# Dealing the projections and filter pieces evenly over the attention steps of a two-block kernel

## The chip, the cores and the metric

The kernel runs on one core of one Trainium2 chip. The metric is the device time of one execution in microseconds (us). Before the change three runs took 1946.99, 1946.99 and 1947.81 us, a median of 1946.99 us. The execution that the profiler took lasted 1947.53 us, with a span of 1945.8 us from the first to the last instruction.

## The reference

Four layers run in sequence over 512 tokens of width 1024: two layers of a first block and two of a second. The change touches the first block alone, so both of its layers. One such layer computes:

```python
h = rms_norm(x, pre_norm[l], NORM_EPS)
q, k, v, z_a, u_h, z_h, g_a, g_h = jnp.split(h @ w_in[l], splits, axis=-1)
o = diff_attention(q, k, v, lam, rel_bias)          # 4 heads, softmax(c=0) - lam * softmax(c=1)
o = rms_norm(o, subln[l], SUBLN_EPS) * (1.0 - lam_init)
y_a = o * silu(z_a)
hv, hx1, hx2 = jnp.split(short_conv3(u_h, conv_w[l], conv_b[l]), 3, axis=-1)
filt = hyena_filters(S, ...)                        # a small sine network, then a spectrum
z = fft_long_conv(hv, filt[:, 0], bias0) * hx1
z = fft_long_conv(z, filt[:, 1], bias1) * hx2
y_h = z * silu(z_h)
m = sigmoid(g_a) * (y_a @ w_pa[l]) + sigmoid(g_h) * (y_h @ w_ph[l])
x = x + rms_norm(m @ w_out[l], post_norm[l], NORM_EPS)
```

Two things matter here. The columns of `h @ w_in` are independent of one another, and so are the filters, so both can be computed at any time before they are used. The gates `sigmoid(g_a)` need neither the attention nor the convolution.

## The kernel before

Matmuls are done in three passes on split operands (`mm3`, L261 to L263): a high and a low part of each side. A projection of 128 columns (`projT`) is therefore 8 x 3 = 24 matmuls of 128x512, and its weights come through `wchunk`: a DMA on SP's queue into one of two buffers `wr` (L283), a copy to `wh` on ACT (L269) and the remainder to `wl` on DVE, or on POOL for every third one (L270).

`attention1` walks over 16 steps: 4 heads `hd` times 4 query tiles `i`. A step computes the logits of its two softmaxes into `lg` (L669, L670, two buffers), adds the bias and takes the row maximum on DVE (L673), negates it (L677), takes exponentials on ACT (L679), and combines the two on DVE (L682 to L686) into a weight tile `p`. The transposes of `p` (L586), their copy `wt` on ACT (L588) and the product with the values (`av`, L590) are kept in the list `later` and issued one step afterwards. After a head's fourth step `finish` normalises the head: squares on ACT (L634), a small sum on DVE (L636), a power on POOL (L637), a product on DVE (L638), four transposes on PE (L641), the gating on DVE (L642), and the split of the result into `yh` and `yl` (L269 on ACT, L270 on POOL).

Beside these steps three generators are advanced, one `next` at a time:

- `filters` (called `flt`): for each of four groups (o, g) four pieces with small matmuls (L505, L506) and two pieces of `bank` products, 24 pieces in all, plus three at the start that are taken before the attention. Every group ends in four stores `hd` on SP's queue (L558, L559).
- `proj(hd)` (called `nxt`): the key and the query projection of the next head and the gate `z_a` of this head, three pieces; only the gate for the last head. The keys and queries of head 0 are made before the first step.
- `hyena_v` (called `zv`): a first `next` that only allocates `z`, then four projections with a short convolution (L710 to L712), then four gate projections with one ACT pass each (L837). What is left of it runs after the last step.

`NX[i]` is the number of `nxt` pieces in query tile `i`; `ZS` lists, by step number `4 * hd + i`, when `zv` is advanced.

Behind the attention come `hyena` (two long convolutions through transforms: sums and differences L751 to L755, transposes L761, forward products into `lg`, elementwise work L784 to L801, inverse products L820), and, dealt into it, `branch_a`: products of `w_pa` with `y_a`, in the order of the heads, added on DVE at L854.

The text order of the Python code is not the order on the engines. The tile framework replays the program on its own timeline and writes out one order for each engine; each engine then runs its list strictly in order, so that an instruction that waits holds up all that is behind it on that engine. PSUM has two `acc` buffers, one `fl`, two `lg`, one `tr`, one `ft` and one `av`.

Of the kernel before, what the change touches and what calls it, by code (L numbers as in the profile page):

```python
# [171 lines left out]
class Kern:  # L172
# [389 lines left out]
    def attention1(self, l, h, v, flt, zv):  # L562
# [19 lines left out]
        def values(hd, i, w, po):  # L582
            def run():
                pw = self.ps("tr", (P, 4, P))
                for kt in range(4):
                    nc.tensor.transpose(pw[:, kt], w[:, kt * P:(kt + 1) * P], self.ident)  # L586
                wt = self.T("wt", (P, 4, P))
                nc.scalar.activation(wt, pw, AF.Copy)  # L588
                for kt in range(4):
                    nc.tensor.matmul(po[:, i], wt[:, kt], v[:, kt, hd * P:(hd + 1) * P],  # L590
                                     start=kt == 0, stop=kt == 3)
            return run
# [32 lines left out]
        def finish(hd, po, s0):  # L625
            def run():
                za = gate[hd]

                e0 = self.sm(4, "e0")
                nc.vector.scalar_tensor_tensor(e0, s0, 1e-5, s0, op0=MUL, op1=MUL)  # L630
                ss = self.sm(4, "hss")
                o = self.T("o", (P, 4, P))
                for i in range(4):
                    nc.scalar.activation(o[:, i], po[:, i], AF.Square, accum_out=ss[:, i:i + 1])  # L634
                r = self.sm(4, "hr")
                nc.vector.scalar_tensor_tensor(r, ss, 1.0 / P, e0, op0=MUL, op1=ADD)  # L636
                nc.gpsimd.tensor_tensor(r, r, self.mhalf[:, :4], op=ALU.pow)  # L637
                nc.vector.tensor_tensor(o, po, self.bc(r), op=MUL)  # L638
                pt = self.ps("tr", (P, 4, P))
                for i in range(4):  # L640
                    nc.tensor.transpose(pt[:, i], o[:, i], self.ident)  # L641
                nc.vector.scalar_tensor_tensor(za, pt.rearrange("p i t -> p (i t)"), subs, za, op0=MUL, op1=MUL)  # L642
                self.split(za, yh[:, hd], yl[:, hd], pool=True)
            return run
# [4 lines left out]
            nc.gpsimd.memset(la[b].bitcast(F32), 0.0)  # L649
            nc.gpsimd.memset(lb[a].bitcast(F32), 0.0)  # L650

        NX, ZS = (1, 2, 0, 0), (8, 12, 13, 14, 15)
        for _ in proj(-1):
            pass
        for hd in range(4):
            nxt = proj(hd)
            bias = self.bias_tile(hd)
            po = self.ps("av", (P, 4, P))
            s0 = self.sm(4, "s0")
            for i in range(4):  # L660
                ts = slice(i * P, (i + 1) * P)
                for _ in range(2):
                    next(flt, None)
                mx, s = self.sm(2, "mx"), self.sm(1, "s1")
                pp = []
                for c in range(2):
                    q, k, kl = qk[hd][c]
                    ps = self.ps("lg")
                    nc.tensor.matmul(ps, q[:, ts], k, start=True, stop=False)  # L669
                    nc.tensor.matmul(ps, q[:, ts], kl, start=False, stop=True)  # L670
                    p = self.T("p")
                    b0 = 511 + 128 * i
                    nc.vector.tensor_tensor_reduce(  # L673
                        out=p, in0=ps, in1=bias[:, b0:b0 - S if i else None:-1], op0=ADD, op1=MAX,
                        scale=1.0, scalar=-3.0e38, accum_out=mx[:, c:c + 1])
                    pp.append(p)
                nc.vector.tensor_scalar(mx, mx, -1.0, None, op0=MUL)  # L677
                for c in range(2):
                    nc.scalar.activation(pp[c], pp[c], AF.Exp, bias=mx[:, c:c + 1],  # L679
                                         accum_out=s0[:, i:i + 1] if c == 0 else s)  # L680
                r1 = self.sm(1, "r1")
                nc.vector.reciprocal(r1, s)  # L682
                cc = self.sm(1, "cc")
                nc.vector.scalar_tensor_tensor(cc, s0[:, i:i + 1], nlam, r1, op0=MUL, op1=MUL)
                w = pp[0]
                nc.vector.scalar_tensor_tensor(w, pp[1], cc, w, op0=MUL, op1=ADD)  # L686
                for f in later:
                    f()
                for _ in range(NX[i]):
                    next(nxt, None)  # L690
                for _ in range(ZS.count(4 * hd + i)):
                    next(zv)
                later = [values(hd, i, w, po)] + ([finish(hd, po, s0)] if i == 3 else [])
# [922 lines left out]
```

## Time and profile before

| | |
|---|---|
| median of 3 runs | 1946.99 us |
| profiled execution | 1947.53 us, span 1945.8 us |
| PE busy | 1882.4 us (97%) |
| PE weight loads busy | 1566.2 us (80%) |
| DVE busy | 1290.4 us (66%) |
| ACT busy | 890.0 us (46%) |
| POOL busy | 648.2 us (33%) |
| chain that ended last | PE 65%, DVE 11% |

PE is the engine that is nearly always busy; the other four are not. The shares are means over the whole span. For a change that touches two stretches of it (the attention of layer 0, 60 to 200 us, and that of layer 1, 530 to 680 us), the views by stretch tell more: they give the busy time of each engine, the number of instructions, the TensorE clock that was granted (1.00 is the full 2.4 GHz, 0.50 would be 1.2 GHz throughout) and the share of the DMA engines.

### The profile page before, as it was taken

What the parts mean: (1) busy time and instruction counts of PE and PEld (TensorE: products, weight loads), DVE (VectorE), ACT (ScalarE), POOL (GpSimd) and SP (SyncE); (2) the same over time, 40 slices, a digit from 0 to 9 for tenths busy, and PEclk for the clock granted to TensorE, in tenths of its full rate; (3) what the DMA queues carried; (4) which work ended last, traced back from release to release, by engine and by line L of the source; (5) the groups of instructions that cost most, each with busy time, mean ns of one, the idle gap of its engine ahead of it and who ended that gap; (6) DMA issues with size and microseconds to landing.
All of it is one profiled execution on the core that took longest, in us unless ns stands there. A gap on an engine that the chain in (4) does not pass through costs nothing.

```text
span 1945.8 us, 26168 instructions
## 1 busy us (share of the span) xinstructions
PE 1882.4 (97%) x9632; PEld 1566.2 (80%) x9632; DVE 1290.4 (66%) x2278; ACT 890.0 (46%) x1732; POOL 648.2 (33%) x555
## 2 busy tenths in 40 slices
PE   8997999999998899999999999999999999999998
PEld 5886888888787687888888777788889887778886
DVE  5887698634697868873558866667334886666732
ACT  4765322234475632233346254466334625446631
POOL 2544344433243634442235314211013532421111
PEclk9999999999999999999999999999999999999999
DMA  5331433324323242323432231112333223121232
GB/s 180 106 121 64 146 109 98 105 91 163 117 86 113 73 170 89 112 93 104 135 123 75 81 101 39 63 44 77 138 127 107 75 87 95 38 63 47 83 130 87
DMA packets 88393, 192.35 MB, mean 99 GB/s; under 512 B 28258, under 2 KB 38499, under 8 KB 88265
## 3 DMA queue, kind: packets, MB, share of 16 engines
q1 hardware_dynamic: 69592, 184.84, 29.0%
q10 hardware_dynamic: 17376, 3.67, 1.0%
q0 software_dynamic: 1296, 2.16, 0.4%
q8 instruction: 76, 1.25, 0.3%
q14 instruction: 53, 0.43, 0.1%
HBM read 172.28 MB, written 18.37 MB: 98 GB/s over the span
## 4 chain that ended last, share of the span: by engine, by line
PE 65%; DVE 11%; issue 3%; ACT 2%; DMA 1%; POOL 1%; ACTq 1%; POOLq 0%; DVEq 0%; SPq 0%
PE acc L261 11%; PE acc L263 11%; PE acc L262 11%; PE fl L261 5%; PE fl L262 5%; PE fl L263 5%; PE av L1166 2%; DVE u L1373 1%; DVE s L1371 1%; PE av L261 1%; PE av L262 1%; PE av L263 1%; PE lg L1470 1%; DVE wl L270 1%; PE av L820 1%
## 5 line engine op out<-in xcount | busy, mean ns | idle before, releaser
L269 ACT ACTIVATE wh<-wr 128x1024 fp32r<-128x1024 f32 (+3 forms) x268 | 256.1, 956 | 467.5 <-PE acc L262 231.3
L261 PE MATMUL acc<-u,wh 128*128 128x512 f32 x1000 | 400.6, 401 | 3.2 <-DVE o L704 1.9
L262 PE MATMUL acc<-u,wh 128*128 128x512 f32 x1000 | 400.4, 400 | 0.0
L263 PE MATMUL acc<-u,wl 128*128 128x512 f32 x1000 | 397.8, 398 | 0.0
L270 POOL TENSOR_TENSOR wl<-wr,wh 128x1024 fp32r<-128x1024 f32 (+3 forms) x86 | 187.2, 2177 | 555.2 <-ACT wh L269 460.2
L270 DVE TENSOR_TENSOR wl<-wr,wh 128x1024 fp32r<-128x1024 f32 (+3 forms) x182 | 213.3, 1172 | 184.8 <-ACT wh L269 182.6
L261 PEld LDWEIGHTS acc<-u,wh 128*128 128x128 f32 x1000 | 190.8, 191 | 46.1 <-issue 3.3
L263 PEld LDWEIGHTS acc<-u,wl 128*128 128x128 f32 x1000 | 190.9, 191 | 43.6 <-issue 4.9
L262 PEld LDWEIGHTS acc<-u,wh 128*128 128x128 f32 x1000 | 190.8, 191 | 39.8 <-issue 2.3
L261 PE MATMUL fl<-u,wh 128*128 128x512 f32 x312 | 124.4, 399 | 0.0
L263 PE MATMUL fl<-u,wl 128*128 128x512 f32 x312 | 122.7, 393 | 0.0
L262 PE MATMUL fl<-u,wh 128*128 128x512 f32 x312 | 122.2, 392 | 0.0
L263 PE MATMUL acc<-wh,u 128*128 128x512 f32 (+1 forms) x212 | 79.3, 374 | 0.3
L262 PE MATMUL acc<-wl,u 128*128 128x512 f32 (+1 forms) x212 | 79.4, 374 | 0.0
L261 PE MATMUL acc<-wh,u 128*128 128x512 f32 (+1 forms) x212 | 77.8, 375 | 0.4 <-ACT u L269 0.2
L261 PEld LDWEIGHTS fl<-u,wh 128*128 128x128 f32 x312 | 58.7, 188 | 12.8 <-issue 1.6
L679 ACT ACTIVATE p<-p,mx 128x512 f32<-128x512 f32 x64 | 45.7, 717 | 49.9 <-DVE mx L677 49.9
L263 PEld LDWEIGHTS fl<-u,wl 128*128 128x128 f32 x312 | 58.6, 188 | 12.1
L262 PEld LDWEIGHTS fl<-u,wh 128*128 128x128 f32 x312 | 58.7, 188 | 12.0 <-issue 0.8
L324 ACT ACTIVATE sq<-x 128x512 f32<-128x512 f32 x40 | 25.2, 631 | 61.4 <-DVE x L1569 38.4
L793 POOL TENSOR_TENSOR w<-w,ab 128x256 f32<-128x256 f32 x32 | 33.5, 1047 | 57.9 <-DVE w L792 53.1
L902 POOL TENSOR_TENSOR m<-m,u 128x512 f32<-128x512 f32 x16 | 24.7, 1546 | 66.3 <-DVE m L901 66.3
(610 smaller groups left out, 4473.8 us busy)
## 6 DMA issues: line engine op xcount, KB each, us to landing
wr<-in_win SPq DMA_DIRECT2D x88, 512.0 KB, 3.4
wr<-in_xin SPq DMA_DIRECT2D x64, 512.0 KB, 3.4
wr<-in_xout SPq DMA_DIRECT2D x32, 512.0 KB, 3.5
hd<-f SPq DMA_DIRECT2D x32, 256.0 KB, 2.4
hs<-hd SPq DMA_DIRECT2D x32, 256.0 KB, 3.4
wr<-in_wout SPq DMA_DIRECT2D x16, 512.0 KB, 3.5
xd<-x SPq DMA_DIRECT2D x12, 512.0 KB, 2.9
x<-xd SPq DMA_DIRECT2D x12, 512.0 KB, 3.9
```

The source lines that it names most:

```text
L261: mm(ps, l[0], r[0], start=first, stop=False)
L262: mm(ps, l[0], r[1], start=False, stop=False)
L263: return mm(ps, l[1], r[0], start=False, stop=last)
L269: nc.scalar.activation(hi, src, AF.Copy)
L270: (nc.gpsimd if pool else nc.vector).tensor_tensor(lo, src, hi.bitcast(F32), op=SUB)
L324: self.nc.scalar.activation(self.T("sq"), self.xt(i)[:, h * S:(h + 1) * S], AF.Square, scale=1.0 / math.sqrt(D), accum_out=self.ms2[i][:, ...
L679: nc.scalar.activation(pp[c], pp[c], AF.Exp, bias=mx[:, c:c + 1], accum_out=s0[:, i:i + 1] if c == 0 else s)
L793: nc.gpsimd.tensor_tensor(a[:, 0], a[:, 0], b[:, 1], op=ADD)
L820: nc.tensor.matmul(ps[:, k], Y[j][:, k, cs], iv[:, j, (k + 1) // 2 % 2], start=j == 0, stop=j == 1)
L902: nc.gpsimd.tensor_tensor(m, m, ma[f // 4][:, f % 4], op=ADD)
L1166: mm(po[:, ts], v[hd // 4][:, k, (hd % 4) * P:(hd % 4 + 1) * P], w[:, k], start=k == 0, stop=k == i)
L1371: nc.vector.tensor_tensor(t, a[:, j, c:].unsqueeze(2).to_broadcast([64, r, c]), m[:, j:j + 1, :c].to_broadcast([64, r, c]), op=MUL)
```

## The change

Three tuples of numbers change. With `NX = (1, 1, 1, 0)` each of the first three query tiles of a head gets one of the three projections (key, query, gate), where the second tile used to get two. With the new `ZS` the four convolution projections go to steps 3, 7, 11 and 13, and two of the four gate projections to steps 14 and 15; the other two still follow the last step. So each of the 16 steps now holds exactly one projection of 24 matmuls. `FS = (2, 1, 2, 1)` deals six filter pieces, one whole group, to each head, where two pieces a step used to use up all 24 in steps 0 to 11.

```diff
-        NX, ZS = (1, 2, 0, 0), (8, 12, 13, 14, 15)
+        NX, ZS, FS = (1, 1, 1, 0), (3, 3, 7, 11, 13, 14, 15), (2, 1, 2, 1)
         for _ in proj(-1):
             pass
         for hd in range(4):
@@
             for i in range(4):
                 ts = slice(i * P, (i + 1) * P)
-                for _ in range(2):
+                for _ in range(FS[i]):
                     next(flt, None)
```

What this makes of the engines' lists is shown at three places. The first is PE in layer 0, between the logits of steps 10 and 11 (head 2). `lg` are logits, `av` the values' product, `fl` and `ft` filter sums, `acc` a projection. Before:

```order
L669 MATMUL lg_1632<-qk_1025,qk_1145 128x512
L670 MATMUL lg_1632<-x_246,qk_1145 128x512
L669 MATMUL lg_1637<-qk_1026,qk_1146 128x512
L670 MATMUL lg_1637<-x_246,qk_1146 128x512
L590 MATMUL av_913<-v_292,wt_1394 128x128 x4
L505 MATMUL fl_1198<-fwh_1186,a_46_255 128x256
L505 MATMUL ft_1212<-fwh_1186,a_46_255 128x256
L669 MATMUL lg_1713<-qk_1025,qk_1145 128x512
L670 MATMUL lg_1713<-x_246,qk_1145 128x512
```

The same place now, without the repeated rows of the projection `acc_1597` and of the filter sums:

```order
L669 MATMUL lg_1568<-qk_1032,qk_1112 128x512
L670 MATMUL lg_1568<-x_246,qk_1112 128x512
L669 MATMUL lg_1573<-qk_1033,qk_1113 128x512
L670 MATMUL lg_1573<-x_246,qk_1113 128x512
L261 MATMUL acc_1597<-u_94,wh_1599 128x512
...
L505 MATMUL fl_1450<-fwh_1321,a_46_255 128x256
...
L590 MATMUL av_908<-v_292,wt_1385 128x128 x4
L505 MATMUL ft_1528<-fwh_1321,a_46_255 128x256
...
L669 MATMUL lg_1663<-qk_1032,qk_1112 128x512
L670 MATMUL lg_1663<-x_246,qk_1112 128x512
```

Between the two steps' logits stood one product with the values and two filter matmuls; now a whole projection of 24 matmuls stands there with eight filter matmuls and the product with the values.

The second place is PE in layer 1 at the end of the attention: the last product with the values, and the transposes of `finish` for head 3 (`tr<-ident,o`). Before, with `acc_6061` and `acc_6126` as projections:

```order
L590 MATMUL av_5844<-v_4399,wt_6165 128x128 x4
L261 MATMUL acc_6061<-u_4092,wh_6063 128x512
...
L263 MATMUL acc_6126<-u_4093,wl_6129 128x512
L641 MATMUL tr_6183<-ident,o_6174 128x128 x4
L261 MATMUL acc_6192<-u_4092,wh_6194 128x512
```

Now, with `acc_6409` and `acc_6460` as branch products with head 3 of `y_a`, and `lg_6369` as the first forward product of the convolution:

```order
L263 MATMUL fl_6474<-u_4093,wl_6477 128x512
L590 MATMUL av_5828<-v_4399,wt_6187 128x128 x4
L586 MATMUL tr_6225<-ident,p_6167 128x128 x4
L761 MATMUL ft_6594<-ident,qd_6585 128x128 x2
L761 MATMUL ft_6594<-ident,qd_6591 128x128 x2
L590 MATMUL av_5828<-v_4399,wt_6230 128x128 x4
L641 MATMUL tr_6248<-ident,o_6239 128x128 x4
L761 MATMUL tr_6358<-ident,qd_6342 128x128 x2
L761 MATMUL tr_6358<-ident,qd_6348 128x128 x2
L261 MATMUL acc_6409<-u_4538,wh_6404 128x512
L261 MATMUL acc_6460<-u_4538,wh_6404 128x512
L261 MATMUL lg_6369<-sd_6337,x_6331 128x256
```

48 matmuls of two projections (and twelve filter matmuls) stood between the last product with the values and the transposes, and 96 more of four projections behind them; now the transposes follow the product directly, and the branch products that need them follow after four transposes.

The third place is SP's queue in layer 0 at the same point: `x` is the next layer input, loaded into the buffers that the filters' tables leave, `hd` the last filter stores, `wr` weights, `hs` the first filter loads of the convolution. Before:

```order
L283 DMA wr_2189<-in_win 128x1024
L915 DMA x_3926<-in_x 128x1024 x2
L558 DMA hd_223<-f_1701 128x512
L559 DMA hd_225<-f_1677 128x512
L558 DMA hd_224<-f_1706 128x512
L559 DMA hd_226<-f_1678 128x512
L283 DMA wr_2303<-in_wpa 128x1024
L770 DMA hs_2265<-hd_219 128x512
```

And now:

```order
L283 DMA wr_2189<-in_win 128x1024
L283 DMA wr_2303<-in_wpa 128x1024
L283 DMA wr_2375<-in_win 128x1024
L915 DMA x_3926<-in_x 128x1024
L283 DMA wr_2428<-in_win 128x1024
L915 DMA x_3926<-in_x 128x1024
L558 DMA hd_223<-f_2052 128x512
L559 DMA hd_225<-f_1964 128x512
L558 DMA hd_224<-f_2057 128x512
L559 DMA hd_226<-f_1965 128x512
L283 DMA wr_2545<-in_wpa 128x1024
L770 DMA hs_2265<-hd_219 128x512
```

Three weight loads moved ahead of the input load and the filter stores.

## Rows read from the trace of the kernel before

**Rows 1.** The page's first part: busy us, share of the span, instructions.

```profile
span 1945.8 us, 26168 instructions
...
PE 1882.4 (97%) x9632; PEld 1566.2 (80%) x9632; DVE 1290.4 (66%) x2278; ACT 890.0 (46%) x1732; POOL 648.2 (33%) x555
```

**Rows 2.** Busy time by stretch of the span; the first line names the columns.

```profile
core 0: us, PE busy (x) PEld busy (x) DVE busy (x) ACT busy (x) POOL busy (x), PEclk, DMA share, GB/s
60.00:130.00 70.00, 70.00 (x378) 60.15 (x377) 61.48 (x118) 47.39 (x94) 36.53 (x32) 1.00 0.32 107
130.00:200.00 70.00, 53.98 (x285) 45.02 (x284) 54.16 (x106) 39.96 (x92) 34.18 (x32) 0.90 0.25 81
250.00:330.00 80.00, 76.86 (x409) 65.14 (x408) 74.99 (x108) 20.46 (x27) 38.62 (x30) 1.00 0.31 99
530.00:570.00 40.00, 40.00 (x206) 32.76 (x205) 35.35 (x68) 29.37 (x52) 14.91 (x15) 1.00 0.27 91
570.00:680.00 110.00, 95.05 (x522) 79.36 (x521) 92.70 (x171) 67.69 (x157) 54.72 (x51) 0.97 0.27 88
```

**Rows 3.** Timeline of PE, layer 0: start, length, instruction, idle before it.

```profile
158.17 0.47 PE L669 MATMUL lg<-qk,qk 128*128 128x512 f32 x1 [1.74 <-DVE mx L673]
...
173.78 0.51 PE L669 MATMUL lg<-qk,qk 128*128 128x512 f32 x1 [3.06 <-DVE mx L673]
...
175.57 0.79 PE L261 MATMUL acc<-u,wh 128*128 128x512 f32 x1 [0.86 <-DVE o L704]
...
180.43 0.63 PE L263 MATMUL acc<-u,wl 128*128 128x512 f32 x1
180.85 0.45 PE L261 MATMUL acc<-u,wh 128*128 128x512 f32 x1
...
181.37 0.39 PE L263 MATMUL acc<-u,wl 128*128 128x512 f32 x1
181.60 0.39 PE L261 MATMUL acc<-u,wh 128*128 128x512 f32 x1
```

**Rows 4.** Timeline, layer 1, from the last product with the values to head 3's split.

```profile
672.95 1.05 PE L590 MATMUL av<-v,wt 128*128 128x128 f32 x8
...
674.04 0.28 ACT L634 ACTIVATE o<-av 128x128 f32<-128x128 f32 x1 [0.29 <-PE av L590]
...
675.95 0.88 DVE L636 SCALAR_TENSOR_TENSOR hr<-hss,e 128x4 f32<-128x4 f32 x1
...
676.90 1.40 POOL L637 TENSOR_TENSOR hr<-hr,mhalf 128x4 f32<-128x4 f32 x1
...
678.34 0.69 DVE L638 TENSOR_TENSOR o<-av,hr 128x512 f32<-128x512 f32 x1
...
686.70 0.60 PE L641 MATMUL tr<-ident,o 128*128 128x128 f32 x4
...
687.91 0.74 DVE L642 SCALAR_TENSOR_TENSOR o<-tr,subs,o 128x512 f32<-128x512 f32 x1
...
688.68 0.63 ACT L269 ACTIVATE u<-o 128x512 fp32r<-128x512 f32 x1 [0.29 <-DVE o L642]
...
690.22 1.47 POOL L270 TENSOR_TENSOR u<-o,u 128x512 fp32r<-128x512 f32 x1
```

**Rows 5.** The same in layer 0, to the product on DVE.

```profile
217.33 1.06 PE L590 MATMUL av<-v,wt 128*128 128x128 f32 x8
...
220.19 2.37 DVE L636 SCALAR_TENSOR_TENSOR hr<-hss,e 128x4 f32<-128x4 f32 x1
...
224.17 0.69 DVE L638 TENSOR_TENSOR o<-av,hr 128x512 f32<-128x512 f32 x1 [0.93 <-POOL hr L637]
```

**Rows 6.** Groups on DVE, 55 to 700 us: count, busy us, mean ns, idle before.

```profile
L270 DVE TENSOR_TENSOR u<-f,u 128x512 fp32r<-128x512 f32 x32 | 32.5, 1026 | 1.0 <-ACT u L269 0.7
...
L557 DVE TENSOR_TENSOR f<-f,f 128x512 f32<-128x512 f32 x16 | 18.1, 1156 | 2.9 <-POOL f L556 2.9
```

**Rows 7.** Timeline of DVE, layer 0: two splits of a filter tile.

```profile
128.92 0.69 DVE L270 TENSOR_TENSOR u<-f,u 128x512 fp32r<-128x512 f32 x1
...
187.24 2.82 DVE L270 TENSOR_TENSOR u<-f,u 128x512 fp32r<-128x512 f32 x1
```

**Rows 8.** SP's own queue, end of layer 0's attention: start, length, issue.

```profile
189.54 16.20 SPq L283 DMA_DIRECT2D wr<-in_win  x2
208.39 0.81 SPq L915 DMA_DIRECT2D x<-in_x  x2
...
214.16 0.45 SPq L283 DMA_DIRECT2D wr<-in_wpa  x1
```

## The prediction

> **What bounds the kernel now.** I read the first part of the page first: PE is busy for 97% of the span, DVE for 66% [rows 1]. So only what PE loses can be won, some 63 us in all, and the question is how much of that lies where the change works. The view by stretch answers it [rows 2]. In the first half of layer 0's attention (60 to 130 us) PE has no gap. In the second half (130 to 200 us) it is busy for 53.98 of 70 us and the granted clock is 0.90. Layer 1 repeats this: full from 530 to 570 us, then 95.05 of 110 us from 570 to 680 us at a clock of 0.97. The reader is to see that one attention has two unlike halves, and that no other engine is full in the poor half: DVE is busy for 54.16 of 70 us there. The timeline of PE shows what a gap looks like [rows 3]: logits that wait for the row maximum of the step before (idle 1.74 and 3.06 us), with nothing else in PE's list to go on with. And it shows what follows a gap: the projection that begins at 175.57 us runs at first with 0.42 us from one matmul to the next (180.43 to 180.85 us) and from then on with 0.23. That is the clock at 1.2 GHz and at 2.4 GHz; the twelve spacings up to 180.85 us took 5.28 instead of 12 x 0.23 = 2.76 us, so this slow stretch cost 2.5 us.
>
> **What is there to win.** Idle: 70 - 53.98 = 16.0 us in layer 0 and 110 - 95.05 = 15.0 us in layer 1. Clock: a mean of 0.90 over 70 us is 2 x 0.10 x 70 = 14 us at half clock, of which half is lost while PE is busy, 7 x 0.77 = 5.4 us; in layer 1 2 x 0.03 x 110 = 6.6 us at half, 3.3 x 0.86 = 2.8 us. Sum: 31.0 + 8.2 = 39.2 us [rows 2]. Nothing that PE computes is removed, so this is the ceiling of the gain.
>
> **Part one: the steps themselves.** The moved work is matmuls that need no attention result. At 0.23 us (the full-clock spacing) a projection is 24 x 0.2275 = 5.5 us. Before, steps 2, 3, 6, 7, 10 and 11 issue none and steps 1, 5, 9 and 12 issue two; now every step has one, and between the logits of steps 10 and 11 PE's list has 24 projection matmuls where it had two filter matmuls and one product with the values. PE's work in layer 0's attention is 70 + 53.98 - 5.4 = 118.6 us, plus the two gates that move in, 2 x 5.5 = 10.9 us: 129.5 us, 8.1 us a step. DVE has 61.48 + 54.16 = 115.6 us, plus at most two weight remainders of some 1.3 us: 118.2 us, 7.4 us a step. So PE becomes the slower of the two in every step, by 0.7 us, and a gap needs a delay beyond that. The halves that are dense already show how close this can go: DVE at 61.48 of 70 us (88%) and at 35.35 of 40 us (88%), with PE full both times [rows 2]. Now DVE must hold 118.2 / 129.5 = 91%. Bounds: if it can, no idle is left; if it stops at 88%, the stretch takes 118.2 / 0.88 = 134.3 us and leaves 4.8 us. I take the middle, 2.4 us a layer, 4.8 us for both.
>
> What moves with a projection: its weight load on SP's queue, its copy on ACT, its remainder on DVE or POOL. ACT is at 39.96 of 70 us and POOL at 34.18 [rows 2], so these stay hidden; if that cover went, a weight chunk would stand 1 to 2 us late before one projection. The filter pieces are spread to steps 12 to 15 and with them the last four stores, which the second convolution alone needs, tens of us later. On SP's queue the old order made the branch weights wait behind the input load and the stores, from 208.39 to 214.16 us [rows 8]; now they stand ahead of both, and behind the waiting input load stands one weight load, for a projection after the first forward products. I take 0 for this; between 0 and 1 us.
>
> **Part two: the end of the attention.** Here the change adds waits. The gates that moved were PE's work while head 3 was finished. After the last product with the values (672.95 to 674.0 us) the squares start at 674.04 and the product on DVE ends at 679.03 us, 5.0 us later; the transposes waited in PE's own list until 686.70 [rows 4], 13.7 us after the product began, and nobody minded. From the transposes' start to the end of the copy (688.68 + 0.63) are 2.6 us more, and the low part on POOL took 1.47 us. In layer 0 the first part took from 218.39 to 224.86, 6.5 us [rows 5], since DVE's small sum took 2.37 us.
>
> Now in layer 1's list the transposes come directly behind the last product. PE will stand for about 5.0 us (3 at the least: four squares of 1.2, then 0.2, 1.0 and 0.7; 6.5 at the most, as in layer 0). Queued behind them on PE are four transposes (0.35 us), two branch products with head 3 and the forward products of the convolution; DVE's gating and all of the convolution's elementwise work wait for those. The branch products then wait 2.6 - 0.35 = 2.2 us for head 3's high part, and the next ones some 0.3 us (up to 1.6) for the low part. Before the last product PE waits 0.3 to 0.6 us for the copy of its transposes. Sum 7.8 us. Behind so long a stand I expect the half clock, as behind the 3.06 and 0.86 us of rows 3: 2.5 us. Layer 1 pays 10.3 us (6 to 13).
>
> In layer 0 the list has eight projection matmuls and four transposes between the last product and the transposes of `finish`: 1.8 + 0.35 = 2.2 us of cover. So 5.0 - 2.2 = 2.8 us, then the same 2.2 and 0.3 us, and the half clock half the time, 1.3 us: 6.6 us (2 to 10).
>
> On that half clock the Trainium skill says the same in a stronger form ("TensorE: Matmul & The Clock Gate", section "Part 1: The HAM clock gate"): the slow clock is the default state, and only activity releases it. By that rule the stand in layer 1 costs its 2.5 us for certain, and the sum stays; if the clock held, the forecast would be some 4 us lower. Rows 3 agree with it.
>
> **Part three: the convolution behind it.** Its first forward products used to come after 26 (layer 0) and 28 (layer 1) branch and projection matmuls of this stage; now 44 come first in both, which leaves 18 and 16 matmuls less to run beside its elementwise chain: 4.1 and 3.7 us. From 250 to 330 us DVE is busy for 74.99 of 80 us while PE already loses 3.1 us [rows 2], so cover has worth there. Bounds 0 and 7.8 us; I take half, 3.9 us, since DVE also gets two or three of its instructions done earlier.
>
> **The sum.** Won 39.2; paid back 4.8 + 10.3 + 6.6 + 3.9 = 25.6. Net 13.6 us: 1947.5 - 13.6 = 1933.9 us against the profiled execution, which stands 0.5 us above the median. Against the median 1933.4 us.
>
> **The rivals.**
>
> *The end is covered after all.* If DVE and ACT are well ahead of PE at the last step, and the finish takes 3 us, layer 0 has no stand (3.0 - 2.2 = 0.8) and the clock holds in both; paid back are then 2.4 us between the steps, 0.5 + 3.0 + 2.2 + 0.3 = 6.0 at layer 1's end, 0.8 + 2.2 + 0.3 = 3.3 at layer 0's and nothing in the convolution, 11.7 us: 1947 - 27.5 = 1919 us. For it: PE is now the slower engine in every step, so the others run ahead. Against it: the chain was 5.0 and 6.5 us long in the two cases that the trace has [rows 4, 5].
>
> *DVE becomes the bound.* The moved filter pieces bring POOL's sums and DVE's two-operand instructions into the half with three heads to finish. Such instructions stretch beside POOL: the split of a filter tile took 0.69 us once and 2.82 us another time, with a mean of 1.03 over 32; the sixteen differences had a mean of 1.16 [rows 6, 7]. The excess is 32 x 0.34 + 16 x 0.47 = 18 us for both layers. If it doubled, 9 us a layer would put DVE at 127 of 129.5 us, and the gaps between steps would come back at half their size, 19.6 us: 39.2 - 19.6 - (25.6 - 4.8) = -1 us, no change, about 1948 us. The skill's rule speaks for this rival: "GPSIMD Engine Reference", section "1. Specifications", has GpSimd share its SBUF interfaces with VectorE and names two-input instructions as those that contend. The rows agree that it happens; they don't show that moving the pieces makes more of it. Against the rival: the first half held 16 of the 24 pieces with PE full.
>
> *The end costs more than the steps give: slower.* One place, the end of each attention: after the last product PE has only work that waits for head 3. At its upper bounds layer 1 loses 0.6 + 6.5 + 2.2 + 1.6 + 2.5 = 13.4 us and layer 0 2.2 less, 11 us, and the convolution its whole 7.8 us, 32 us in all. This decides when the steps win less than 32 of the 39.2 us; with half of them won it is 1947 + 32 - 19.6 = 1959 us. For it: PE's list of layer 1 has nothing between the last product and the transposes. Against it: the lists give layer 0 eight matmuls, and the steps look dense.
>
> **How the numbers follow.** The forecast 0.58 (its own range 1924 to 1943 us), the covered end 0.22, DVE as the bound 0.13, the costly end 0.07. The range, 1918 to 1945 us, leaves out the best half of the second case, most of the third and the fourth. About 0.2% (3.9 us) is what a measurement of this kernel tells from no change: below 1943.1 us lie the forecast, the second case and a little of the third: faster 0.85; same 0.09; slower 0.06.
>
> **What would show it.** Right: from 130 us to the end of layer 0's attention, and from 570 us in layer 1, logits no longer wait 1 to 3 us for the maximum and the clock is 1.00; PE stands 3 to 6 us at the transposes of `finish` at the end of layer 1's attention, less in layer 0, with a dip of the clock behind it. Wrong: logits that still wait inside heads 1 to 3 (DVE bound), or no stand at the two ends (then it is faster than I say), or new idle of over 4 us a layer inside the convolution.

## The result, and the profile after

The changed kernel takes 1932.85 us (median of 4 runs, 1931.28 to 1934.41); the kernel before took 1946.99 us on the same chip (4 runs, 1946.33 to 1947.81). The ratio is 0.9927, 95% interval 0.9910 to 0.9944. The forecast was 1933.4 us. The profiled execution lasted 1933.28 us, 14.3 us less than the one before.

The first part of the page, beside [rows 1]: the same matmuls on PE, the same busy time, a shorter span.

```profile
span 1931.5 us, 26186 instructions
...
PE 1882.2 (97%) x9632; PEld 1565.8 (81%) x9632; DVE 1294.6 (67%) x2278; ACT 890.4 (46%) x1732; POOL 653.9 (34%) x555
```

The stretches of [rows 2] again; the columns are those named there (length, busy us of PE, its weight loads, DVE, ACT and POOL, granted clock, DMA):

```profile
60.00:130.00 70.00, 68.40 (x368) 57.55 (x368) 63.17 (x114) 46.44 (x94) 33.17 (x30) 1.00 0.29 99
130.00:200.00 70.00, 68.78 (x380) 58.28 (x379) 60.35 (x112) 44.76 (x96) 39.74 (x35) 1.00 0.36 116
250.00:330.00 80.00, 74.24 (x381) 63.13 (x380) 68.75 (x101) 18.23 (x24) 38.26 (x30) 0.94 0.31 99
...
570.00:680.00 110.00, 103.87 (x550) 87.63 (x549) 93.59 (x158) 66.75 (x142) 60.16 (x52) 0.97 0.36 118
```

The second half of layer 0's attention, where PE was busy for 53.98 of 70 us at a clock of 0.90, is now dense at 1.00. The convolution behind it lost: 74.24 of 80 us at 0.94, where it was 76.86 at 1.00. And layer 1's stretch is better only by half.

To see where the time went, the same view cut at the work's own marks: from the first to the last logits, on to the first forward product of the convolution, on to its last inverse product; layer 0, then layer 1. Before:

```profile
60.20:185.10 124.90, 113.55 (x612) 96.66 (x611) 102.17 (x206) 78.31 (x171) 57.85 (x52) 0.96 0.30 99
185.10:241.90 56.80, 52.13 (x266) 43.81 (x265) 37.57 (x56) 24.40 (x45) 24.72 (x20) 0.97 0.42 135
241.90:375.80 133.90, 130.76 (x687) 111.25 (x686) 113.89 (x160) 36.41 (x49) 60.83 (x48) 1.00 0.33 107
535.20:659.60 124.40, 113.01 (x604) 94.71 (x602) 105.97 (x204) 81.87 (x175) 56.85 (x51) 0.97 0.28 92
659.60:716.20 56.60, 53.04 (x276) 44.17 (x275) 39.23 (x64) 25.23 (x46) 21.61 (x19) 1.00 0.43 149
716.20:852.80 136.60, 132.51 (x686) 112.81 (x685) 113.95 (x160) 36.27 (x48) 62.97 (x48) 0.98 0.32 105
sum 633.20, PE 595.00 PEld 503.42 DVE 512.77 ACT 282.48 POOL 284.82; mean PE 99.17 PEld 83.90 DVE 85.46 ACT 47.08 POOL 47.47
```

After:

```profile
60.10:192.40 132.30, 129.48 (x703) 109.22 (x702) 116.55 (x216) 87.30 (x183) 68.19 (x61) 1.00 0.32 106
192.40:230.40 38.00, 35.82 (x196) 30.00 (x194) 24.05 (x45) 16.11 (x34) 11.47 (x9) 1.00 0.49 158
230.40:367.80 137.40, 130.39 (x665) 110.92 (x665) 115.75 (x161) 35.55 (x48) 63.22 (x49) 0.96 0.32 104
527.40:663.00 135.60, 129.76 (x687) 109.26 (x686) 118.38 (x219) 90.55 (x187) 67.88 (x57) 0.97 0.31 102
663.00:707.50 44.50, 39.63 (x212) 33.08 (x210) 27.53 (x49) 18.13 (x37) 15.44 (x13) 0.94 0.46 148
707.50:841.10 133.60, 130.15 (x665) 110.96 (x665) 116.34 (x161) 35.59 (x47) 63.02 (x49) 0.97 0.31 103
sum 621.40, PE 595.24 PEld 503.45 DVE 518.61 ACT 283.22 POOL 289.22; mean PE 99.21 PEld 83.91 DVE 86.43 ACT 47.20 POOL 48.20
```

The first column after the stretch is its length, so length minus PE is what PE stood:

| PE idle, us | before | after |
|---|---|---|
| layer 0: steps / end / convolution | 11.4 / 4.7 / 3.1 | 2.8 / 2.2 / 7.0 |
| layer 1: steps / end / convolution | 11.4 / 3.6 / 4.1 | 5.8 / 4.9 / 3.4 |
| sum | 38.2 | 26.2 |

The six stretches are 11.8 us shorter, and that is the idle time alone: PE's busy sum is the same (595.00 and 595.24 us). The clock gave nothing. Time at half clock, 2 x (1 - clock) x length summed over views of 10 us up to 960 us, was 27 us and is 31 us; it left layer 0's steps and came back in the convolutions and at layer 1's end. Of the other 2.5 us of the 14.3, 2.3 lie in layer 2 (485.3 us from its first transposes to layer 3's, now 483.0), where the engines' lists are the same in both kernels. The four runs of experiments 1 to 4, also with that list, took 484.2 to 485.8 us for it: that part is scatter, not the change.

The largest stand left between the steps, on PE, then on DVE (the second of its two differences once more by itself), then on POOL (start, length, instruction, idle before it):

```profile
649.40 0.79 PE L669 MATMUL lg<-qk,qk 128*128 128x512 f32 x1 [4.49 <-DVE mx L673]
```

```profile
644.23 4.51 DVE L557 TENSOR_TENSOR f<-f,f 128x512 f32<-128x512 f32 x2
...
645.91 2.83 DVE L557 TENSOR_TENSOR f<-f,f 128x512 f32<-128x512 f32 x1
...
648.66 0.68 DVE L673 CUSTOM_DVE_ANT_0 p<-lg,bias 128x512 f32<-128x512 f32 x1
```

```profile
642.91 2.53 POOL L556 TENSOR_TENSOR f<-f,f 128x512 f32<-128x512 f32 x2 [6.94 <-DVE f L552]
645.40 2.79 POOL L270 TENSOR_TENSOR wl<-wr,wh 128x1024 fp32r<-128x1024 f32 x1
```

Logits wait for a row maximum, as in [rows 3], and the maximum stands behind two filter differences in DVE's list, which took 4.51 us. The same pair in the kernel before stood at 657.69 us:

```profile
657.69 2.36 DVE L557 TENSOR_TENSOR f<-f,f 128x512 f32<-128x512 f32 x2
```

So it did not move into the late heads; it became 2.15 us longer, since POOL, when it had done its two sums, now had a weight remainder to make beside the second difference. The rows show how. The second difference ended at 648.74 us, 0.55 us after POOL's remainder (645.40 + 2.79 = 648.19). All eight of the sixteen differences of this trace that took over 0.7 us began while POOL was in an instruction of L556 or L270 and ended 0.55 us after it; the other eight took 0.67 to 0.69 us. So the difference looks held until POOL is done, not slowed, and the row maximum behind it in DVE's list waited for POOL too.

And the end of layer 1's attention, beside [rows 4], on PE and on the two engines that its chain had been slow on:

```profile
699.25 1.16 PE L590 MATMUL av<-v,wt 128*128 128x128 f32 x8 [0.31 <-ACT wt L588]
703.76 1.08 PE L641 MATMUL tr<-ident,o 128*128 128x128 f32 x4 [3.35 <-DVE o L638]
705.69 1.11 PE L761 MATMUL tr<-ident,qd 128*128 128x128 f32 x4 [0.84 <-DVE o L642]
```

```profile
701.62 0.16 DVE L636 SCALAR_TENSOR_TENSOR hr<-hss,e 128x4 f32<-128x4 f32 x1 [2.28 <-ACT o L634]
701.87 1.03 POOL L637 TENSOR_TENSOR hr<-hr,mhalf 128x4 f32<-128x4 f32 x1 [19.99 <-DVE hr L636]
702.93 0.69 DVE L638 TENSOR_TENSOR o<-av,hr 128x512 f32<-128x512 f32 x1 [1.14 <-POOL hr L637]
```

The transposes of `finish` stand for 3.35 us, and not 5: from the end of the last product (700.41 us) to the end of the product on DVE (703.62) are 3.2 us, where [rows 4] had 5.0. The small sum took 0.16 us instead of 0.88, the power 1.03 instead of 1.40, and the sum began 1.2 us after the last product's end instead of 1.95.

### The profile page after: what moved, and what is told of

Read it like the earlier page. It is cut to its first block, busy times and chain, and to the rows that moved or that the text cites. A ratio compares the mean times of both kernels' runs of the same rounds, so it can differ in the third digit from the quotient of the medians.

```text
span 1931.5 us, 26186 instructions
## 1 busy us (share of the span) xinstructions
PE 1882.2 (97%) x9632; PEld 1565.8 (81%) x9632; DVE 1294.6 (67%) x2278; ACT 890.4 (46%) x1732; POOL 653.9 (34%) x555
## 4 chain that ended last, share of the span: by engine, by line
PE 52%; DVE 6%; ACT 1%; issue 1%; POOL 1%; DMA 1%; ACTq 1%; POOLq 0%; DVEq 0%
PE acc L263 8%; PE acc L262 8%; PE acc L261 8%; PE fl L261 4%; PE fl L262 4%; PE fl L263 4%; PE av L1166 2%; DVE u L1373 2%; DVE s L1371 1%; PE av L262 1%; PE av L261 1%; PE av L263 1%; PE lg L1470 1%; PE lg L1462 1%; DVE wl L270 1%
## 5 line engine op out<-in xcount | busy, mean ns | idle before, releaser
L270 POOL TENSOR_TENSOR wl<-wr,wh 128x1024 fp32r<-128x1024 f32 (+3 forms) x86 | 186.4, 2168 | 510.9 <-ACT wh L269 422.1
L270 DVE TENSOR_TENSOR wl<-wr,wh 128x1024 fp32r<-128x1024 f32 (+3 forms) x182 | 210.4, 1156 | 165.9 <-ACT wh L269 164.9
```

Of the source, the lines that this page charges most:

```text
L270: (nc.gpsimd if pool else nc.vector).tensor_tensor(lo, src, hi.bitcast(F32), op=SUB)
```

## The experiments

The experiments were timed in four groups, 1 to 4, 5 to 8, 9 to 11 and 12, each with the kernel before beside them; it took 1948.53, 1945.99, 1947.29 and 1947.21 us there, so across the groups the ratios count. "Steps", "end" and "convolution" are the stretches above. The theory at the start: the gain is the projections that fill the empty steps; the two moved gates uncover the attention's end; the filter dealing costs and brings nothing.

**1. The gates back behind the loop.**

```diff
-ZS = (3, 3, 7, 11, 13, 14, 15)
+ZS = (3, 3, 7, 11, 13)
```

> The changed kernel with steps 14 and 15 taken out of ZS again: all four gate projections stand behind the last step in the text, as before the change; the even dealing of projections and filter pieces stays. By the prediction the two moved gates are what uncovered the end of each attention (10.3 us in layer 1, 6.6 in layer 0): with them back, the stand of PE at the transposes of `finish` (5 us in layer 1) should be gone and steps 14 and 15 should have idle again; the sum is somewhere from 1922 to 1940 us, and the two traces must differ at the end of the attention. Rival: the framework's replay takes the gates forward to the same places whether ZS names them or not. PE's list of this kernel differs from that of the changed one in 12 rows of some 7800, all between steps 13 and 16 of layer 1; then the time is that of the changed kernel, 1932.9 us within 2 us, and the stands at the end are the same.

Measured 1932.71 us (1931.87 to 1933.39), ratio 0.9921 (0.9908 to 0.9935): the changed kernel's time. Its longest waits of PE (us in total, times, longest):

```profile
PE lg L669 <- DVE mx L673: 5.8, 4, 4.5
PE av L820 <- DVE e L822: 5.8, 2, 4.6
PE tr L641 <- DVE o L638: 5.4, 3, 3.4
```

The changed kernel has 5.8 (4, 4.5), 5.8 (2, 4.7) and 5.7 (3, 3.4) there. So naming the two gates in `ZS` does nothing: the replay puts them in nearly the same places when the text has them behind the last step.

**2. The filter dealing alone**, on the kernel before.

```diff
-for _ in range(2):
+for _ in range(FS[i]):     # FS = (2, 1, 2, 1), old NX and ZS
```

> The kernel before with one part of the change: FS = (2, 1, 2, 1), the old NX and ZS. By the prediction the gain comes from the projections that fill the steps, and filter pieces are too short to fill one (eight small matmuls): 1947 us within 4 us, with the waits for the row maximum in steps 6 to 12 of both layers still there. Rival: what counts is that each step has PE work of any kind and that DVE is unloaded in the first twelve steps; then half the gain or more is here, 1940 us or less.

Measured 1940.40 us (1938.38 to 1943.22), ratio 0.9961 (0.9948 to 0.9973): 8.1 us faster, where the theory had nothing. The waits between the steps are still there (PE busy 106.85 of 118.1 us in layer 0); the gain is in layer 0's end, which has no idle where before had 4.7 us:

```profile
178.20:235.50 57.30, 57.30 (x298) 48.77 (x297) 36.97 (x65) 27.43 (x50) 25.80 (x20) 0.98 0.39 134
```

298 matmuls stand in that stretch, 266 before. The 32 more are not filter pieces: 26 of them are projections (185 for 159), and of the 32 filter matmuls of L505 in this layer 28 stand ahead of the last logits in both kernels. So the new dealing hardly moved the filter pieces on PE. It changed what the replay makes of the rest: the last logits come at 178.2 us instead of 185.1, and one projection more is left behind them. The theory's third sentence is wrong. The rival's time came, but not its reason, since the steps kept their idle time.

**3. The projections alone.**

```diff
-FS = (2, 1, 2, 1)
+FS = (2, 2, 2, 2)     # new NX and ZS
```

> The changed kernel with the old filter dealing, two pieces in every step (FS = (2, 2, 2, 2)): the projections alone are dealt evenly. By the prediction this holds the gain: 1933 us within 4 us, the second half of the attention dense. Rival: without the filters spread, steps 0 to 11 hold a projection and two filter pieces each, so DVE is late there and the gaps come back in the first heads, while steps 12 to 15 have too little: 1940 us or more.

Measured 1927.42 us (1924.68 to 1928.97), ratio 0.9890 (0.9875 to 0.9905). The projections bring 21 us; on top of them the filter dealing costs some 5 us. Layer 1's stretches:

```profile
530.30:656.60 126.30, 122.45 (x656) 104.15 (x655) 109.22 (x212) 86.77 (x172) 59.97 (x51) 0.97 0.31 105
656.60:703.30 46.70, 44.53 (x243) 37.64 (x241) 31.34 (x56) 23.20 (x52) 20.42 (x19) 1.00 0.43 140
703.30:833.90 130.60, 128.31 (x666) 109.25 (x666) 115.66 (x161) 35.66 (x48) 61.93 (x49) 0.99 0.32 110
```

They take 303.6 us with 8.3 us of idle (the changed kernel 313.7 with 14.2); layer 0 takes 310.4 against 307.7. So the new filter dealing helps layer 0 and hurts layer 1. Other profiles agree: with the changed kernel's dealing layer 0 takes 305.6 and 306.2 us in experiments 1 and 10, and layer 1 takes 312.5 us in experiment 1.

**4. The last two gates held on PE** behind the last product with the values.

```diff
-            self.gate(l, h, 32 + f, ma[0][:, f])
+            with self.after(self.av if f > 1 else None):
+                self.gate(l, h, 32 + f, ma[0][:, f])
```

> The changed kernel, with the matmuls of the last two gate projections ordered behind the last product with the values on PE (an order on PE alone, nothing else changes): 38 projection matmuls stand between that product and the transposes of `finish` in layer 0 and 42 in layer 1, where the changed kernel has 8 and none. By the prediction's mechanism the end of the attention is then covered. The trace of the changed kernel has some 4.5 us of idle, 0.8 to 1.3 us at the branch products and some 2 to 3 us of half clock there in layer 1, and 2.2 us in layer 0: 9 us less, 1924 us (1921 to 1928). Rival: the two projections are then missing in the last steps, which become as thin as before the change, and logits wait there again; what the end wins the steps lose, 1933 us or more.

Measured 1927.76 us (1927.26 to 1930.63), ratio 0.9899 (0.9886 to 0.9913): 5 us less than experiment 1, a little over half of the 9 expected. Layer 1's end, and its last product with the values and the transposes of `finish`, which now follow 10.5 us later without a wait:

```profile
658.90:699.00 40.10, 36.15 (x199) 30.34 (x198) 26.25 (x50) 17.19 (x37) 15.89 (x13) 1.00 0.44 151
```

```profile
677.68 1.16 PE L590 MATMUL av<-v,wt 128*128 128x128 f32 x8 [0.75 <-ACT wt L588]
...
688.23 0.60 PE L641 MATMUL tr<-ident,o 128*128 128x128 f32 x4
```

The stand is gone, and the half clock behind it (1.00 for 0.94). But the last four products with the values, which have no projection beside them any more, now wait 0.7 to 1.4 us each for their copies: 4.0 us of idle instead of 4.9. Layer 0's end, where 2.2 us were to be won, has 3.6. Most of the idle came back a little earlier; what the cover saved for good is clock, and idle in layer 0's convolution (3.9 us for 7.0). Up to layer 2 this trace has 24 us of idle and 17 us at half clock, experiment 1's 26 and 20.

**5. Experiments 3 and 4 together.**

> Both edits that helped, together: projections dealt as in the changed kernel, filter pieces two a step as before (the run with the projections alone took 1927.4 us), and the last two gate projections ordered behind the last product with the values (which won 5.1 us on the changed kernel). If the two gains lie in different stretches they add: 1922.3 us (1919 to 1925), and this beats both kernels and both single edits. Rival: the run with the projections alone has less to cover at the two ends (its trace has 2.91 and 0.84 us of idle there in layer 0, 1.09 and 1.07 us in layer 1), so holding the gates wins 2 us at most: 1925.5 us or more.

Measured 1924.92 us (1923.65 to 1926.14), ratio 0.9891 (0.9878 to 0.9905): experiment 3's ratio. The gains don't add. Layer 0's end improved (idle 3.8 to 1.7 us), layer 1's convolution got worse (idle 2.3 to 4.1).

**6. NX alone**, on the kernel before.

```diff
-NX = (1, 2, 0, 0)
+NX = (1, 1, 1, 0)     # old ZS and FS
```

> The kernel before with one part of the change: NX = (1, 1, 1, 0), old ZS and FS. It puts a projection into steps 2, 6 and 10; steps 3, 7 and 11 still have none. If every step without a projection costs about the same, half of what the projections win together (1948.5 to 1927.4 us) is here: 1938 us (1935 to 1941), and the ends of the attention, which stay covered by projections in PE's list (36 matmuls in layer 0, 43 in layer 1), show no stand. Rival: the gaps sit at the last step of a head, where `finish` and the next head's first logits meet; then this part alone wins little, 1944 us or more.

Measured 1945.24 us (1942.78 to 1947.69), ratio 0.9996 (0.9987 to 1.0005): nothing, as the rival had it. Layer 0's steps still lose 13.1 us, at 0.96:

```profile
60.20:184.00 123.80, 110.67 (x604) 93.94 (x603) 107.99 (x203) 80.23 (x171) 60.66 (x59) 0.96 0.30 100
```

Its layer 0 has no idle at the end of the attention, as in experiment 2; what that won the steps lost (13.1 us for 11.4).

**7. ZS alone.**

```diff
-ZS = (8, 12, 13, 14, 15)
+ZS = (3, 3, 7, 11, 13)     # old NX and FS
```

> The kernel before with the other part: the convolution projections at steps 3, 7, 11 and 13, old NX and FS, gates not named. Steps 2, 6 and 10 have no projection, 1, 5 and 9 have two. PE's list has no projection between the last product with the values and the transposes of `finish` in either layer, as in the changed kernel, so this run pays the ends. If each filled step wins about the same and the ends are paid: 1939 us (1935 to 1943), with a stand of 2 to 4 us at the transposes of `finish` and a dip of the clock behind it. Rival: the convolution projections are the whole of it and the key and query order does not matter: 1929 us or less.

Measured 1934.77 us (1933.38 to 1939.43), ratio 0.9949 (0.9935 to 0.9962): some 10 us. Its layer 0:

```profile
60.20:191.00 130.80, 127.90 (x711) 110.09 (x710) 114.40 (x221) 88.48 (x185) 68.45 (x63) 1.00 0.34 111
```

2.9 us of idle at full clock: the convolution projections at the heads' last steps are enough to fill the steps. Spreading the key, query and gate does nothing by itself (experiment 6), and is worth another 11 us by the ratios (0.9949 to 0.9890) beside them. The ends of this run have 3.8 and 5.0 us of idle, though it names no gate. In the kernel before, the ACT passes that end a projection tell what stood in layer 1 between the last product (672.95 us) and the transposes of `finish` (686.70), L710 for the convolution and L837 for a gate:

```profile
680.74 0.76 ACT L710 ACTIVATE u<-acc,c 128x512 f32<-128x512 f32 x1
687.63 0.76 ACT L710 ACTIVATE u<-acc,c 128x512 f32<-128x512 f32 x1
693.57 0.58 ACT L837 ACTIVATE u<-acc 128x512 f32<-128x512 f32 x1
```

So the cover there was two convolution projections, which `ZS` takes forward; all four gates came later. In layer 0 the cover was gates (L837 at 224.62 and 230.60 us), which move up with the projections ahead of them.

What the runs without idle in the steps have in common is how many projection matmuls PE has between the first and the last logits, counted in the traces (layer 0 / layer 1):

| | projection matmuls | PE idle in the steps, us |
|---|---|---|
| before | 265 / 265 | 11.4 / 11.4 |
| experiment 6, `NX` alone | 241 / 265 | 13.1 / 11.4 |
| experiment 2, `FS` alone | 241 / 265 | 11.3 / 10.3 |
| experiment 7, `ZS` alone | 336 / 313 | 2.9 / 5.1 |
| experiment 3, `NX` and `ZS` | 313 / 313 | 5.8 / 3.8 |
| changed kernel | 341 / 337 | 2.8 / 5.8 |

Only `ZS` brings more of them there. The text's steps are not PE's: in layer 0 of the kernel before, steps 2, 3, 6 and 7 have 10, 17, 18 and 15 projection matmuls on PE although the text gives them none, and steps 10, 12, 13 and 14 have at most one. In the changed kernel steps 12 to 15 have 48, 2, 0 and 28, where the text gives 24 to each.

**8. Filler at the end of layer 1.**

```diff
+with self.after(self.av):
+    for j in range(14):
+        last = nc.tensor.matmul(pz, h[0][0][:, 0:P], h[0][0], start=True, stop=True)
```

> The changed kernel with 14 extra matmuls of 128x512 (3.2 us at 0.23) between the last product with the values of layer 1 and the transposes of `finish`; their result goes into a logits buffer and is read by nobody. They use only time in which PE stood (3.35 us). If the clock falls because PE stands, the stretch behind it (0.66 over 700 to 710 us in the changed kernel's trace) is at 1.00, and the time from the last product to the first forward product is 1.5 to 3 us shorter although PE has more to do. If the clock falls for another reason (it comes as often whatever PE does), the dip is still there and that time is the same or longer by up to 0.5 us. The order inside the convolution changes too, so the whole time is no test: 1928 to 1936 us.

```profile
698.16 1.16 PE L590 MATMUL av<-v,wt 128*128 128x128 f32 x8 [0.31 <-ACT wt L588]
699.08 3.46 PE L699 MATMUL lg<-u 128*128 128x512 f32 x14
702.68 0.63 PE L641 MATMUL tr<-ident,o 128*128 128x128 f32 x4
...
705.50 0.51 PE L261 MATMUL lg<-sd,x 128*128 128x256 f32 x2
```

From the last product to the first forward product are 7.34 us, and 8.25 in the changed kernel (699.25 to 707.50), with 3.46 us more for PE to do. The clock over 700 to 710 us is 1.00 where it was 0.66. With the stand filled this dip is gone, so it does come from the stand; it costs 0.9 us up to here, less than the 1.5 expected at least. The whole kernel took 1933.51 us (1931.94 to 1933.99), ratio 0.9934 (0.9921 to 0.9948): the dips in the convolutions stayed (10 and 7 us at half clock).

**9. Each layer with its better dealing**: layer 0 as in experiment 4, layer 1 as in experiment 3.

> Each layer with what its own trace liked best: layer 0 with the spread filter pieces and the last two gates ordered behind the last product with the values (303.8 us from its first logits to its last inverse product in that run), layer 1 with two filter pieces a step and the gates left to the framework (303.5 us). If the stretches are independent, layer 2 starts at 60.2 + 303.8 + 159.5 + 303.5 + 106.8 = 933.8 us, 5 to 7 us earlier than in the two best runs, and the ratio to before is some 0.986 to 0.987. Rival: what a layer takes depends on where the clock dips fall and on what the layer before leaves, so the sum of the best parts is not kept: ratio 0.989 or more.

Measured 1924.37 us (1924.20 to 1926.15), ratio 0.9882 (0.9865 to 0.9899), not told apart from experiments 3 and 5. Layer 0 kept its 303.7 us; layer 1 took 308.1 instead of 303.5, 4.0 us of it in the convolution. The sum of the best parts is not kept.

**10. The filter differences of layer 1 on POOL.**

```diff
-nc.vector.tensor_tensor(ev[i], ev[i], od, op=SUB)
+(nc.gpsimd if l == 1 else nc.vector).tensor_tensor(ev[i], ev[i], od, op=SUB)
```

> The changed kernel with the filters' difference (L557) of layer 1 moved from DVE to POOL, where the sum beside it (L556) already runs. In the changed kernel two of these differences took 4.51 us on DVE beside POOL and stood in DVE's list ahead of a row maximum: PE stood 4.49 us. If that pair is the cause of the hole, the hole at that step goes, and with it one dip of the clock: layer 1 is 5 to 7 us shorter from first to last logits (135.6 us), ratio to before 0.990. Rival: the row maximum is late because DVE is full in that head anyway; then another DVE instruction takes the place, a hole of over 2 us stays and the ratio is 0.9925 or more.

Measured 1927.93 us (1926.85 to 1930.09), ratio 0.9902 (0.9886 to 0.9918), as expected, though its interval overlaps the changed kernel's. Layer 1's steps and the waits in that place:

```profile
525.80:653.90 128.10, 125.14 (x679) 106.28 (x678) 111.26 (x207) 85.83 (x170) 69.69 (x57) 1.00 0.33 108
```

```profile
641.03 0.50 PE L669 MATMUL lg<-qk,qk 128*128 128x512 f32 x1 [1.58 <-DVE mx L673]
644.94 0.50 PE L669 MATMUL lg<-qk,qk 128*128 128x512 f32 x1 [1.24 <-DVE mx L673]
```

7.5 us shorter (128.1 for 135.6), clock 1.00: the hole of 4.49 us and its dip are gone, two waits of 1.6 and 1.2 us took part of its place. The end behind it has 6.7 us of idle, where the changed kernel has 4.9.

**11. Experiments 9 and 10 together.**

> Both of the above: each layer's own dealing, and layer 1's filter differences on POOL. In layer 1 with two filter pieces a step no hole of 4 us was seen, so there is less to win here: 0 to 3 us below the run without the move. Rival: POOL's own queue (splits of weights, sums) gets 8 differences more and a weight remainder comes late for a projection: the same or up to 3 us above it.

Measured 1929.42 us (1926.58 to 1931.31), ratio 0.9907 (0.9889 to 0.9925): the rival's side, if anything. Where DVE has no such pile-up there is nothing to move away.

**12. The convolution's last product on DVE**, on experiment 9.

```diff
-nc.gpsimd.tensor_tensor(zn[:, ct], y, hx, op=MUL)
+nc.vector.tensor_tensor(zn[:, ct], y, hx, op=MUL)
```

> The mix by layer (ratio 0.9882), and the convolution's last product (zn = y * hx, L829 in the changed kernel) on DVE instead of POOL in both layers. On POOL beside DVE this product took 3.38 us where it should take 1.27, and the next group's sums on DVE wait for it; behind them PE stood 0.84 and 2.62 us in layer 0, 1.29 and 4.03 us in layer 1, each time with a dip of the clock. If the stretched product is the cause, those four stands shrink to below 3 us together and the kernel is 5 to 9 us faster: ratio 0.984 to 0.986. Rival: DVE is busy for some 115 of 134 us in the convolution, and 16 products of 0.7 us more make it the bound there: no gain or up to 4 us slower, ratio 0.988 to 0.990.

Measured 1924.55 us (1922.25 to 1925.68), ratio 0.9886 (0.9870 to 0.9903): no gain. The product itself went from a mean of 1.85 us on POOL to 0.69 on DVE (225 to 370 us), but the stands shrank little. In layer 1:

```profile
739.57 0.49 PE L821 MATMUL av<-iv,Y 128*128 128x128 f32 x2 [1.89 <-DVE e L823]
...
742.97 3.17 PE L821 MATMUL av<-iv,Y 128*128 128x128 f32 x14 [2.91 <-DVE Y L802]
```

With layer 0's 2.92 us they are 7.7 us, where experiment 9 had 8.8. The last of them now waits for the next instructions on DVE (`Y`), layer 0's for the same sums as before (`qd`). The stretched product was not the cause. The ratio is the rival's, but DVE is busy for 235.2 of 270.5 us in the two convolutions, so that DVE is the bound is not shown; what limits the convolution there stays open.

Experiments 3, 5, 9 and 12 beat both kernels, by 1.1 to 1.2% of before; the simplest is experiment 3, the change without its filter dealing.

## Why the prediction was right, and where it was not

The time was right to 0.6 us; of the terms some were, and the errors cancelled. So close a hit is luck; that full steps win more than the uncovered ends cost is what was foreseen and came.

- **What there is to win, 31.0 us of idle:** right as a ceiling (11.4 + 4.7 + 11.4 + 3.6 = 31.1 by the marks). That it goes when steps are filled is shown by experiments 3 and 7. Which steps are empty was read from the text and not from PE: experiment 6 fills three steps of a layer in the text, brings no more projection matmuls between the logits and wins nothing.
- **Between the steps, 2.4 us a layer:** 2.8 in layer 0, 5.8 in layer 1, with DVE busy for 88% and 87% of the stretch, as in the dense halves before, and not for 91%. The mis-sized part is one place, 4.49 us, where the rival "DVE becomes the bound" came true once. As that rival said, it was a filter's difference stretched beside POOL, but not because its piece was moved, and the stretching as a whole did not grow: the two groups of [rows 6] now have means of 0.935 and 1.327 us, 50.7 us together, and had 50.6. Its place, beside a weight remainder on POOL and ahead of a row maximum on DVE, is what cost. The Trainium skill's "GPSIMD Engine Reference", section "1. Specifications", names VectorE instructions with two SBUF inputs as contending with GpSimd; the 4.51 us for a pair that took 2.36 before agree, and so does experiment 10, where the move ended the stand. The argument against this rival was weak: the 16 of 24 pieces in the first half are the text's, and PE had fewer than 12 of them from 60 to 130 us (16 matmuls of L505, which are eight small pieces, and 43 of the 48 `bank` matmuls of the first two groups).
- **The filter dealing, taken as 0 to 1 us: failed.** I looked at SP's queue and took the text's place of a piece for its place on the engines; the pieces stayed nearly where they were, and the replay moved the logits and projections around them. Alone it wins 8.1 us, on top of the projections it costs some 5 (experiments 2 and 3).
- **"The gates that moved were PE's work while head 3 was finished": failed as a cause.** Naming them in `ZS` does nothing (experiment 1). Gates were the cover in layer 0 alone, in layer 1 it was two convolution projections; it went because the convolution projections come earlier, and the gates with them (experiment 7).
- **The two ends, 10.3 and 6.6 us:** too much. Layer 1 stood for 0.31 + 3.35 + 0.84 = 4.5 us, with 0.9 us of clock up to the forward products by experiment 8; that is 5.4 us, below my bounds (6 to 13). Layer 0 stood for 2.2 us at full clock, near its lower bound. The chain of [rows 4, 5] was the wrong price: it was measured where DVE and POOL had other work beside it, and where PE is late they have none. So "the end is covered after all" was nearer at the ends than the forecast was.
- **The clock, 8.2 us won and 3.8 paid: failed.** Nothing was won, as PE's equal busy sums show. Of the time at half clock 10 us came back in the convolution of layer 0, behind its stand of 4.66 us, and 7 us in layer 1. How much of that is due to the change is not settled: experiment 1, with nearly the same lists and as much idle in the six stretches (26.1 us against 26.2), had 20 us at half clock where the changed kernel's profile has 31 (sums over stretches of 10 us up to 960 us). The rule cited from the Trainium skill's "TensorE: Matmul & The Clock Gate", section "Part 1: The HAM clock gate", agrees with experiment 8: with PE kept busy the clock held.
- **The convolution, 3.9 us:** near in sum (3.9 us more idle in layer 0, 0.7 less in layer 1), not in its division.

In idle the sum was 31.0 - 4.8 - 13.1 - 3.9 = 9.2 us won, where 12.0 came; of the clock 4.4, where none came; and 2.3 us of scatter in layer 2 made up for the rest.

## What to carry to other kernels

When a framework writes the engines' lists from a replay, a line of the dealing table is not a place on an engine: count in the trace or in the lists what stands where, since a move may change nothing (the gates), leave its own pieces in place and move others (the filters), or take the cover of something else (the end). Deal each kind of filler by itself and in each stage by itself before dealing all evenly; here the even filter dealing helped one layer, hurt the other, and the change without it was faster. Count a stall's idle time as gain, and not its clock loss, unless the next stall is gone as well.

## What the runs showed of the hardware

The same subtraction of two 128x512 tiles on DVE took from 0.67 to 2.83 us within one execution: each one that began well inside a sum or a weight remainder on POOL ended 0.55 us after that one. A pair of them took 2.36 us with POOL's sum beside the first, and 4.51 with a weight remainder beside the second as well. The time at half clock differs by 10 us between two kernels that stand equally long (31 and 20 us), so a single profile does not settle a clock term of a few us.
